# One-hot columns of 128 built as products of a column of 8 and a column of 16

## The chip, the cores and the metric

The kernel runs on one core of one Trainium2 chip. A core has five engines with a queue of instructions each: TensorE (PE, matmuls), VectorE (DVE), ScalarE (ACT), GpSimd (POOL) and SyncE (SP, which issues DMAs). Within one queue instructions run in order; between engines they wait on semaphores. The metric is the time of one execution on the device in microseconds; less is better. The size of an effect is read against the spread of repeated runs of the same kernel.

## The reference, cut to what matters

The program is one layer of a streaming encoder for 1152 tokens (1024 of a prompt, 128 of samples), 9 blocks of 128 tokens. A mixer (projections, band attention, a recurrent branch) is followed by a feed-forward part that retrieves experts: each token chooses 128 of 16384 single-neuron experts (8 heads of 16), and expert number e is a pair (i1, i2) of 128 by 128.

```
def peer_tokens(xt, wq, keys1, keys2, expert_u, expert_v):
    t = xt.shape[0]
    q = (xt @ wq).reshape(t, PEER_HEADS, 2, HALF_KEY)
    s1 = jnp.einsum('thd,hnd->thn', q[:, :, 0], keys1).astype(jnp.float32)
    s2 = jnp.einsum('thd,hnd->thn', q[:, :, 1], keys2).astype(jnp.float32)
    v1, i1 = lax.top_k(s1, TOPK_HALF)
    v2, i2 = lax.top_k(s2, TOPK_HALF)
    cand_s = (v1[..., :, None] + v2[..., None, :]).reshape(t, PEER_HEADS, TOPK_HALF * TOPK_HALF)
    cand_i = (i1[..., :, None] * N_KEYS + i2[..., None, :]).reshape(t, PEER_HEADS, TOPK_HALF * TOPK_HALF)
    top_s, pos = lax.top_k(cand_s, TOPK)
    e_idx = jnp.take_along_axis(cand_i, pos, axis=-1)
    g = jax.nn.softmax(top_s, axis=-1)
    u_sel = expert_u[e_idx]
    act = jax.nn.gelu(jnp.einsum('thkd,td->thk', u_sel, xt).astype(jnp.float32))
    return jnp.einsum('thk,thkd->td', (g * act).astype(xt.dtype), expert_v[e_idx])
```

## The kernel before

The token blocks go through the mixer in three groups, `GROUPS = ((0, 1, SB), (2, 3, 4), (5, 6, 7))`, each with five stages: the recurrent branch, its gates, the attention, the output projections, the retrieval scores. Projections take 24 matmuls each with weights split in a high and a low part; from the second group on the low part comes back from DRAM (lines 163 and 164), so DVE no longer makes it there.

The experts are then applied in two ways. Blocks 0, 5, 6, 7 (`GATHER`) fetch rows of the experts by indirect DMA, one per token and choice (line 910), and DVE takes a dot product (line 937) or adds a scaled row (line 958). Blocks 1, SB, 2, 3, 4 (`DENSE`) run all 16384 experts as matmuls at the end (`dense`), masked by a matrix `G_d` in DRAM that holds each token's weight for each expert. `build_g` makes this matrix; the change is in it.

For one token the matrix of 128 by 128 weights is a product of two sets of one-hot columns: choice k gives a column with a one at i1 and a column with its weight at i2. The table of a block (`tab`: i1, i2 and the weight in three factors `pw`, `hi`, `lo`, with choices on the partitions and tokens along the row) is made by `tables`, stored to DRAM and read back into one buffer. `build_g` handles a block in 4 chunks `c` of 32 tokens, and a chunk in 4 parts `tb` of `OH_T = 8` tokens. A part makes three tiles of 128x1024 (8 tokens of 128 columns), `ow`, `oh` and `ol`, with five DVE instructions, lines 993 to 997:

```
V.tensor_tensor(ow, gp["iota"], row(i2), op=ALU.is_equal)
V.tensor_tensor(ow, ow, row(pw), op=ALU.mult)
V.tensor_tensor(oh, gp["iota"], row(i1), op=ALU.is_equal)
V.tensor_tensor(ol, oh, row(lo), op=ALU.mult)
V.tensor_tensor(oh, oh, row(hi), op=ALU.mult)
```

A 128x1024 tile is laid out as groups of two tokens, 128 columns each, with the two tokens of a group side by side in memory; `row` reads a pair of tokens from the table again for every column. PE multiplies the tiles token by token into PSUM (lines 1008 and 1009), ACT copies the product to a staging tile `st` (line 1011), and after four parts SP stores `st` (2 MB) to `G_d` (line 1013). The three tiles have two buffers each, `st` has one. There are 5 blocks of 4 chunks of 4 parts, 80 parts in all.

Where the parts run is set by a queue `fill` of small steps: in the second and third group `beat` takes steps from it after each projection or attention unit, and likewise steps of the gather of block 0 (`FLOW`). The selection steps of the next blocks (lines 766 to 863, all on DVE) go through the same queue. The order of each engine's instructions is fixed at build time by a list scheduler that goes by a modelled time line. In the attention, one unit on DVE is the bias added to the scores (line 432), their maximum `mx` (line 434) and the reciprocal of the sum (line 439); ACT makes `p` from the maximum (line 437) and scales it by the reciprocal (line 443), and PE's next score matmul (line 524) needs the buffer that line 437 has read.

Of the kernel before, what the change touches and what calls it, by code (L numbers as in the profile page):

```python
# [53 lines left out]
OH_T = 8  # L54
# [15 lines left out]
def kernel(ctx, tc, a):  # L70
# [43 lines left out]
    s_d = [dr_p.tile([8, 128, len(g), 2, 128], F32, name=f"s_d{n}") for n, g in enumerate(GROUPS)]  # L114
    e_d = {b: dr_p.tile([128, 128], I32, name=f"e_d{b}") for b in GATHER}
    g_d = {b: dr_p.tile([128, 128], F32, name=f"g_d{b}") for b in GATHER}
    tab_d = {b: dr_p.tile([128, 320], F32, name=f"tab_d{b}") for b in DENSE}
    x2_d = {b: dr_p.tile([128, D], F32, name=f"x2_d{b}") for b in range(NB)}

    def rstd_of(ss, q_="", r=None):  # L120
        m = sm_p.tile([128, 1], F32, name="rs_m" + q_)
        V.tensor_scalar(m, ss, 1.0 / D, EPS, op0=ALU.mult, op1=ALU.add)
        if r is None:
            r = sm_p.tile([128, 1], F32, name="rs_r" + q_)
        S.activation(r, m, ACTF.Sqrt)
        V.reciprocal(r, r)
        q = sm_p.tile([128, 1], F32, name="rs_q" + q_)
        V.tensor_tensor(q, r, r, op=ALU.mult)
        V.tensor_tensor(q, q, m, op=ALU.mult)
        V.tensor_scalar(q, q, -0.5, 1.5, op0=ALU.mult, op1=ALU.add)  # L130
        V.tensor_tensor(r, r, q, op=ALU.mult)
        return r

    def ssq(x, junk, q_=""):
        ss = sm_p.tile([128, 1], F32, name="ss" + q_)
        S.activation(junk, x, ACTF.Square, accum_out=ss)  # L136
        return ss

# [611 lines left out]

    def table_parts(tab):
        h = tab.bitcast(F16)
        return h[:, 0:128], h[:, 128:256], tab[:, 128:192].bitcast(BF16), h[:, 384:512], h[:, 512:640]

    def select(b, q_=""):

# [119 lines left out]
        def tables(ii, gf):  # L876


            pt = ps_p.tile([128, 4, 128], F32, name="tr", tag="pp")
            for n, src in enumerate((ii[0], ii[1], gf)):  # L880
                T.transpose(pt[:, n, :], src, ident)
            tab = tk.tile([128, 320], F32, name="tab", tag="cand")
            i1, i2, pw, hi, lo = table_parts(tab)
            S.copy(i1, pt[:, 0, :])
            S.copy(i2, pt[:, 1, :])
            wt = tk.tile([128, 128], F32, name="wt", tag="sh")
            S.copy(wt, pt[:, 2, :])
            ma = tk.tile([128, 128], F32, name="ma", tag="m1")
            bits = wt.bitcast(U32)
            V.tensor_scalar(ma.bitcast(U32), bits, 0x007fffff, 0x46000000, op0=ALU.bitwise_and, op1=ALU.bitwise_or)  # L890
            V.tensor_scalar(bits, bits, 0x7f800000, None, op0=ALU.bitwise_and)
            V.tensor_copy(pw, wt)
            S.copy(hi, ma)
            V.tensor_tensor(lo, ma, hi, op=ALU.subtract)
            nc.sync.dma_start(tab_d[b], tab)
# [73 lines left out]
    def build_g(gp, b):  # L969
# [4 lines left out]
        def part(c, tb):  # L974
            def go():
                if c == 0 and tb == 0:
                    make_tables(b)
                    st["t"] = gp["st"].tile([128, 320], F32, name="tab")
                    nc.sync.dma_start(st["t"], tab_d[b])
                if tb == 0:  # L980
                    st["s"] = gp["st"].tile([128, 128, 32], F32, name="st")
                i1, i2, pw, hi, lo = table_parts(st["t"])
                sg = st["s"]
                t = c * 32 + tb * OH_T

                def row(x):
                    return x[:, t:t + OH_T].rearrange("p (g t) -> p g t", t=2).unsqueeze(2).to_broadcast(
                        [128, OH_T // 2, 128, 2])

                ow = gp["oh"].tile([128, OH_T // 2, 128, 2], BF16, name="ow")  # L990
                oh = gp["oh"].tile([128, OH_T // 2, 128, 2], F16, name="oh1")
                ol = gp["oh"].tile([128, OH_T // 2, 128, 2], F16, name="oh2")
                V.tensor_tensor(ow, gp["iota"], row(i2), op=ALU.is_equal)
                V.tensor_tensor(ow, ow, row(pw), op=ALU.mult)
                V.tensor_tensor(oh, gp["iota"], row(i1), op=ALU.is_equal)
                V.tensor_tensor(ol, oh, row(lo), op=ALU.mult)
                V.tensor_tensor(oh, oh, row(hi), op=ALU.mult)
                later.append(lambda: products(c, tb, ow, oh, ol, sg))
                if len(later) > 1:
                    later.popleft()()  # L1000
# [144 lines left out]
    for n, blocks in enumerate(GROUPS):  # L1145
        phase[0] = n
        if n:
            if not gp:
                gp["iota"] = iota = g_p.tile([128, OH_T // 2, 128, 2], F16, name="iota", tag="g5")
                P.iota(iota, pattern=[[0, OH_T // 2], [1, 128], [0, 2]], base=0, channel_multiplier=0,  # L1150
                       allow_small_or_imprecise_dtypes=True)
                gp["st"] = es_g.enter_context(tc.tile_pool(name="st", bufs=1, side="right", reuse_waits="tile"))
                gp["oh"] = es_g.enter_context(tc.tile_pool(name="oh", bufs=2, side="right", reuse_waits="tile"))
            for b in GROUPS[n - 1]:
                if b in DENSE:
# [144 lines left out]
```

## Time and profile before

| what | value |
|---|---|
| median of 3 runs | 3978.68 us (3971.28 to 3997.58) |
| the profiled execution, its own time | 3979.21 us |
| its span, first to last instruction | 3977.3 us |
| busy: PE, PEld (weight loads), DVE, ACT, POOL | 92%, 82%, 77%, 41%, 35% |
| mean granted clock of PE, as a share of 2.4 GHz | 0.967 |
| parts of `build_g` | 80, from 926 to 1994 us |

The span falls into the first group (to about 900 us), the second and third group (to about 2000 us, with all of `build_g` in them) and the dense part with the remaining gathers (to the end). "Busy" is the time in which an engine has an instruction running; waits are listed by the engine that waits and by what it waited for. The granted clock is one of two levels, 1.2 and 2.4 GHz, so a mean of 0.94 says that 12% of the stretch ran at the lower one.

### The profile page before, as it was taken

To read this page: it belongs to the slowest core of one execution; us is meant where nothing else is said; L and a number is where in the kernel's file an instruction comes from. 1 tells how busy PE (TensorE), PEld (TensorE's weight loads), DVE (VectorE), ACT (ScalarE), POOL (GpSimd) and SP (SyncE) were. 2 spreads that over 40 slices of the span, in tenths; PEclk is the share of its full clock that TensorE was granted. 3 is DMA by queue.
4 is the path that set the end of the run, shared out by engine and by line. 5 is a ranking of instruction groups with operands and counts; after the bars stand their busy time and mean duration, and the time that the engine had idled before them with its cause. 6 is when DMAs were issued, how large, how long until landed. Compare 5 with 4: busy or idle time off the path is not lost. (4 is left out here: it accounts for less than half of the span.)

```text
span 3977.3 us, 59539 instructions
## 1 busy us (share of the span) xinstructions
PE 3647.0 (92%) x21775; PEld 3264.7 (82%) x21775; DVE 3042.7 (77%) x6332; ACT 1618.2 (41%) x2699; POOL 1405.4 (35%) x1094
## 2 busy tenths in 40 slices
PE   8998899898998999888888889999999899999998
PEld 7877799876887987778888778888888888888887
DVE  8433357868675879987778888888877887877887
ACT  7554346556644845665532122222222222222222
POOL 0000000122221023222106555655664655655653
PEclk9999999999998999999999999999999999999999
DMA  7778887888899898879968888989888889888986
GB/s 260 253 243 317 296 283 271 327 308 269 316 385 331 294 346 292 292 281 360 379 203 308 306 287 296 320 314 343 311 305 293 322 313 332 311 304 305 331 311 233
DMA packets 470358, 1208.05 MB, mean 304 GB/s; under 512 B 41008, under 2 KB 199088, under 8 KB 467504
## 3 DMA queue, kind: packets, MB, share of 16 engines
q1 hardware_dynamic: 292496, 638.23, 45.2%
q0 software_dynamic: 147456, 536.94, 37.8%
q10 hardware_dynamic: 30112, 29.09, 2.1%
q8 instruction: 170, 2.79, 0.3%
q14 instruction: 124, 1.02, 0.1%
HBM read 1066.15 MB, written 137.94 MB: 303 GB/s over the span
## 5 line engine op out<-in xcount | busy, mean ns | idle before, releaser
L910 POOL DMA_INDIRECT row<-peer_u,ei x512 | 698.0, 1363 | 1260.5 <-DVE row L937 631.3
L910 POOL DMA_INDIRECT row<-peer_v,ei x512 | 683.3, 1334 | 828.7 <-DVE x L958 525.4
L958 DVE SCALAR_TENSOR_TENSOR x<-row,q,x 128x1024 f32<-128x1024 f32 x512 | 655.3, 1280 | 27.2 <-DMA row<-peer_v,ei 20.8
L175 PE MATMUL pp<-xd,hi 128*128 128x320 f32 x2048 | 639.8, 312 | 31.9 <-ACT wf L1043 26.9
L937 DVE SCALAR_TENSOR_TENSOR row<-row,xt 128x1024 f32<-128x1024 f32 x512 | 613.6, 1217 | 66.1 <-DMA row<-peer_u,ei 64.4
L176 PE MATMUL pp<-xd,hi 128*128 128x320 f32 x2048 | 637.5, 311 | 0.3 <-DVE xd L142 0.3
L177 PE MATMUL pp<-xd,lo 128*128 128x320 f32 x2048 | 636.8, 311 | 0.0
L175 PE MATMUL pp<-xn,hi 128*128 128x384 f32 x1344 | 477.4, 356 | 19.1 <-ACT st L1011 7.8
L1069 PE MATMUL S<-vh,wh 128*128 128x512 f32 x1280 | 410.0, 402 | 62.2 <-DVE acc L1077 54.0
L177 PE MATMUL pp<-xn,lo 128*128 128x384 f32 x1344 | 459.4, 343 | 2.1 <-DMA lo<-lo_w_in 2.1
L176 PE MATMUL pp<-xn,hi 128*128 128x384 f32 x1344 | 460.6, 343 | 0.1
L1069 PE MATMUL S<-vh,wl 128*128 128x512 f32 x1280 | 401.1, 402 | 27.6 <-DVE wl L142 27.6
L175 PEld LDWEIGHTS pp<-xd,hi 128*128 128x128 f32 x2048 | 389.9, 190 | 42.6 <-ACT wf L1043 30.7
L141 ACT CAST hi<-raw 128x1024 fp32r<-128x1024 f32 x223 | 233.8, 1049 | 429.0 <-PE pp L176 307.2
L1069 PE MATMUL S<-vl,wh 128*128 128x512 f32 x1280 | 404.0, 397 | 0.0
L176 PEld LDWEIGHTS pp<-xd,hi 128*128 128x128 f32 x2048 | 389.8, 190 | 7.2 <-DVE xd L142 0.6
L177 PEld LDWEIGHTS pp<-xd,lo 128*128 128x128 f32 x2048 | 389.2, 190 | 1.6
L142 DVE TENSOR_TENSOR lo<-raw,hi 128x1024 fp32r<-128x1024 f32 x223 | 271.9, 1220 | 150.1 <-ACT hi L141 134.8
L141 ACT CAST wh<-wf 128x640 fp32r<-128x640 f32 x128 | 93.3, 729 | 616.8 <-DVE wf L1045 583.6
L1069 PEld LDWEIGHTS S<-vh,wh 128*128 128x128 f32 x1280 | 239.3, 193 | 112.3 <-DVE acc L1077 60.9
L163 ACT CAST hi<-raw 128x1024 fp32r<-128x1024 f32 x192 | 200.4, 1047 | 296.5 <-PE pp L176 204.3
L1069 PEld LDWEIGHTS S<-vh,wl 128*128 128x128 f32 x1280 | 246.7, 194 | 84.6 <-DVE wl L142 32.7
(296 smaller groups left out, 6821.7 us busy)
## 6 DMA issues: line engine op xcount, KB each, us to landing
raw<-w_in SPq DMA_DIRECT2D x168, 512.0 KB
raw<-peer_v SPq DMA_DIRECT2D x128, 512.0 KB
raw<-peer_ut SPq DMA_DIRECT2D x127, 512.0 KB
lo<-lo_w_in SPq DMA_DIRECT2D x112, 512.0 KB
G_d<-st SPq DMA_DIRECT2D x20, 2048.0 KB
gt<-G_d SPq DMA_DIRECT2D x32, 1280.0 KB
lo_w_in<-lo SPq DMA_DIRECT2D x56, 512.0 KB
raw<-wq SPq DMA_DIRECT2D x48, 512.0 KB
```

The source lines that it names most:

```text
L141: S.copy(r32(hi), src)
L142: ins = V.tensor_tensor(r32(lo), src, hi, op=ALU.subtract)
L163: S.copy(r32(hi), raw)
L175: T.matmul(out, r32(lh), r32(rh), start=first, stop=False)
L176: T.matmul(out, r32(lh), r32(rl), start=False, stop=False)
L177: T.matmul(out, r32(ll), r32(rh), start=False, stop=last)
L910: P.indirect_dma_start(out=t, out_offset=None, in_=table, in_offset=bass.IndirectOffsetOnAxis(ap=ei[:, j:j + 1], axis=0))
L937: V.scalar_tensor_tensor(u, u, 1.0, xt, op0=ALU.mult, op1=ALU.mult, accum_out=hh[:, j:j + 1])
L958: V.scalar_tensor_tensor(x2, v, q[:, j:j + 1], x2, op0=ALU.mult, op1=ALU.add)
L1069: T.matmul(po[:, m, :], r32(l[:, c1]), r32(r[:, m * 512:m * 512 + 512]), start=(n == 0 and q == 0 and (c == 0 or not held)), stop=(n == EC ...
```

## The change

A number i1 of 0 to 127 is written as 16 times a (0 to 7) plus b (0 to 15). The one-hot column of 128 is the product of a column of 8 at a and a column of 16 at b. `tables` now stores 16 a and b instead of i1 and i2, so `tab` grows from 320 to 448 words a row; the split is integer work on DVE in place of two ACT copies. Once per chunk `build_g` makes the small columns for its 32 tokens in a tile `fac`: four compares and three multiplications by the weight factors, which now go on the columns of 8. Each part makes `ow`, `oh` and `ol` with one product of 128x1024 each. The large counting tile `iota` is replaced by two small ones, and four small statistics tiles get two buffers instead of four.

```
-    tab_d = {b: dr_p.tile([128, 320], F32, name=f"tab_d{b}") for b in DENSE}
+    tab_d = {b: dr_p.tile([128, 448], F32, name=f"tab_d{b}") for b in DENSE}
...
-        m = sm_p.tile([128, 1], F32, name="rs_m" + q_)
+        m = sm_p.tile([128, 1], F32, name="rs_m" + q_, bufs=2)
...
-            tab = tk.tile([128, 320], F32, name="tab", tag="cand")
-            i1, i2, pw, hi, lo = table_parts(tab)
-            S.copy(i1, pt[:, 0, :])
-            S.copy(i2, pt[:, 1, :])
+            tab = tk.tile([128, 448], F32, name="tab", tag="cand")
+            a1, a2, b1, b2, pw, hi, lo = table_parts(tab)
+            for n, (xa, xb) in enumerate(((a1, b1), (a2, b2))):
+                u = tk.tile([128, 128], U32, name="u", tag=("ra", "m3")[n])
+                v = tk.tile([128, 128], U32, name="v", tag="pf")
+                V.tensor_copy(u, pt[:, n, :])
+                V.tensor_scalar(v, u, 15, None, op0=ALU.bitwise_and)
+                V.tensor_copy(xb, v)
+                V.tensor_scalar(u, u, 0x70, None, op0=ALU.bitwise_and)
+                V.tensor_copy(xa, u)
...
                 if tb == 0:
                     st["s"] = gp["st"].tile([128, 128, 32], F32, name="st")
-                i1, i2, pw, hi, lo = table_parts(st["t"])
+
+                    a1, a2, b1, b2, pw, hi, lo = table_parts(st["t"])
+                    st["f"] = fac = g_p.tile([128, 896], F32, name="fac", tag="g5")
+                    h, w = fac.bitcast(F16), fac.bitcast(BF16)
+
+                    def small(x, n):
+                        return x.rearrange("p (g i t) -> p g i t", i=n, t=2)
+
+                    def row(x, n):
+                        return x[:, c * 32:c * 32 + 32].rearrange("p (g t) -> p g t", t=2).unsqueeze(2).to_broadcast(
+                            [128, 16, n, 2])
+
+                    fh, fl, fw = small(h[:, 0:256], 8), small(h[:, 256:512], 8), small(w[:, 512:768], 8)
+                    g1, g2 = small(h[:, 768:1280], 16), small(w[:, 1280:1792], 16)
+                    st["f"] = fh, fl, fw, g1, g2
+                    for n, pairs in ((8, ((fl, a1), (fw, a2))), (16, ((g1, b1), (g2, b2)))):
+                        for o, x in pairs:
+                            V.tensor_tensor(o, gp["iota", n].unsqueeze(1).to_broadcast([128, 16, n, 2]), row(x, n),
+                                            op=ALU.is_equal)
+                    V.tensor_tensor(fw, fw, row(pw, 8), op=ALU.mult)
+                    V.tensor_tensor(fh, fl, row(hi, 8), op=ALU.mult)
+                    V.tensor_tensor(fl, fl, row(lo, 8), op=ALU.mult)
+                fh, fl, fw, g1, g2 = st["f"]
                 sg = st["s"]
-                t = c * 32 + tb * OH_T
-
-                def row(x):
-                    return x[:, t:t + OH_T].rearrange("p (g t) -> p g t", t=2).unsqueeze(2).to_broadcast(
-                        [128, OH_T // 2, 128, 2])
+
+                def product(o, f, g):
+                    gs, full = slice(tb * OH_T // 2, (tb + 1) * OH_T // 2), [128, OH_T // 2, 8, 16, 2]
+                    V.tensor_tensor(o.rearrange("p g (a b) t -> p g a b t", b=16),
+                                    f[:, gs].unsqueeze(3).to_broadcast(full), g[:, gs].unsqueeze(2).to_broadcast(full),
+                                    op=ALU.mult)
...
-                V.tensor_tensor(ow, gp["iota"], row(i2), op=ALU.is_equal)
-                V.tensor_tensor(ow, ow, row(pw), op=ALU.mult)
-                V.tensor_tensor(oh, gp["iota"], row(i1), op=ALU.is_equal)
-                V.tensor_tensor(ol, oh, row(lo), op=ALU.mult)
-                V.tensor_tensor(oh, oh, row(hi), op=ALU.mult)
+                product(ow, fw, g2)
+                product(oh, fh, g1)
+                product(ol, fl, g1)
```

Two places show what becomes of the order. The first is DVE's queue in the attention of the third group, where a chunk's first parts begin. In the names, `x` is the sum of the gather of block 0, `S` the scores, `tab` the table and `fac` the small columns; a number tells one `oh` tile from another. Before:

```order
L434 TENSOR_REDUCE mx<-S 128x1
L993 TENSOR_TENSOR ow<-iota,tab 128x1024
L995 TENSOR_TENSOR oh_18235<-iota,tab 128x1024
L958 SCALAR_TENSOR_TENSOR x_14646<-row,q,x_14646 128x1024
L995 TENSOR_TENSOR oh_18265<-iota,tab 128x1024
L993 TENSOR_TENSOR ow<-iota,tab 128x1024
L994 TENSOR_TENSOR ow<-ow,tab 128x1024
L996 TENSOR_TENSOR oh_18236<-oh_18235,tab 128x1024
L527 MEMSET S 64x64
L958 SCALAR_TENSOR_TENSOR x_14646<-row,q,x_14646 128x1024
L996 TENSOR_TENSOR oh_18266<-oh_18265,tab 128x1024
```

and with the change, where the chunk begins with the set-up (lines 1006 to 1010; line 965 is the gather's add that was line 958):

```order
L142 TENSOR_TENSOR oa<-pp,oa 128x128
L1006 TENSOR_TENSOR fac<-iota_6457,tab 128x256 x2
L1006 TENSOR_TENSOR fac<-iota_6459,tab 128x512 x2
L1009 TENSOR_TENSOR fac<-fac,tab 128x256
L965 SCALAR_TENSOR_TENSOR x_14672<-row,q,x_14672 128x1024
L1008 TENSOR_TENSOR fac<-fac,tab 128x256
L527 MEMSET S 64x64
L1010 TENSOR_TENSOR fac<-fac,tab 128x256
L1016 TENSOR_TENSOR oh_18589<-fac 128x1024
L965 SCALAR_TENSOR_TENSOR x_14672<-row,q,x_14672 128x1024
L1016 TENSOR_TENSOR ow<-fac 128x1024
L432 TENSOR_TENSOR S<-S,bias 128x256
```

The compares of 128x1024 have gone, seven small instructions stand ahead of the chunk's first products, and the gather's adds and the softmax unit's instructions (`S`, `mx`) stand between the pieces as before.

The second place is SP's queue in the output projections of the second group, where the table of the next block is read into its one buffer. `raw` and `lo` are the high and low weights, `G_d<-st` is the store of a finished chunk. Before:

```order
L1013 DMA G_d<-st 128x4096
L164 DMA lo<-lo_w_ba_4883 128x1024
L154 DMA raw<-w_ba 128x1024
L631 DMA tg_d_8098<-tg 128x384
L164 DMA lo<-lo_w_ba_4924 128x1024
L154 DMA raw<-w_ba 128x1024
L631 DMA tg_d_8098<-tg 128x384
L979 DMA tab<-tab_d_128 128x320
```

and with the change:

```order
L986 DMA tab<-tab_d_128 128x448
L154 DMA raw<-w_ba 128x1024
L631 DMA tg_d_8100<-tg 128x384
L164 DMA lo<-lo_w_in_4723 128x1024
L154 DMA raw<-w_ba 128x1024
L631 DMA tg_d_8100<-tg 128x384
L1041 DMA G_d<-st 128x4096
```

The read of the table has moved ahead of the store of the chunk; the last reader of the old table is now the set-up of a block's fourth chunk, where before it was its last part.

On PE nothing is added or removed, and the groups of 16 one-hot matmuls stand at the same projections as before, to within one.

## Rows read from the trace of the kernel before

**Rows 1.** Busy time of each engine in five stretches, their sum; clock, DMA share, GB/s.
```profile
core 0: us, PE busy (x) PEld busy (x) DVE busy (x) ACT busy (x) POOL busy (x), PEclk, DMA share, GB/s
926.00:1060.00 134.00, 120.51 (x818) 98.06 (x817) 109.59 (x241) 85.06 (x162) 30.90 (x29) 0.94 0.80 277
1060.00:1230.00 170.00, 152.56 (x1024) 142.58 (x1021) 117.23 (x235) 85.42 (x126) 34.59 (x33) 0.96 0.98 375
1230.00:1494.00 264.00, 241.79 (x1344) 223.49 (x1344) 194.90 (x726) 154.24 (x239) 36.32 (x33) 0.95 0.89 318
1494.00:1800.00 306.00, 269.76 (x1848) 218.26 (x1847) 272.69 (x643) 191.13 (x366) 83.32 (x75) 0.94 0.83 290
1800.00:1994.00 194.00, 171.81 (x1210) 162.68 (x1211) 144.63 (x302) 100.13 (x135) 41.92 (x33) 0.96 0.97 371
sum 1068.00, PE 956.42 PEld 845.08 DVE 839.04 ACT 615.99 POOL 227.05; mean PE 191.28 PEld 169.01 DVE 167.81 ACT 123.20 POOL 45.41
```

**Rows 2.** Groups on DVE, 926 to 1994 us: count, busy us, mean ns, idle before.
```profile
L995 DVE TENSOR_TENSOR oh<-iota,tab 128x1024 f16<-128x1024 f16 x80 | 54.8, 685 | 52.3 <-PE pg L1008 52.1
...
L997 DVE TENSOR_TENSOR oh<-oh,tab 128x1024 f16<-128x1024 f16 x80 | 54.4, 681 | 0.0
...
L142 DVE TENSOR_TENSOR oa<-pp,oa 128x128 fp32r<-128x128 f32 x37 | 10.5, 284 | 23.1 <-ACT oa L141 23.1
...
L848 DVE TENSOR_TENSOR oh<-oh 128x512 bf16<-128x512 bf16 x16 | 6.6, 415 | 0.0
...
L844 DVE TENSOR_TENSOR oh<-ra,rank 128x1024 bf16<-128x1024 bf16 x8 | 5.4, 678 | 0.0
...
L848 DVE TENSOR_TENSOR oh<-oh 128x256 bf16<-128x256 bf16 x16 | 4.5, 280 | 0.0
...
L142 DVE TENSOR_TENSOR xn<-tr,xn 128x1024 fp32r<-128x1024 f32 x3 | 3.7, 1225 | 15.3 <-ACT xn L141 15.3
...
L890 DVE TENSOR_SCALAR ma<-wt 128x128 uint32<-128x128 uint32 x4 | 0.9, 228 | 2.8 <-ACT wt L887 2.8
...
L829 DVE CAST rb<-sh 128x128 bf16<-128x128 uint32 x3 | 0.7, 219 | 0.0
```

**Rows 3.** The same stretches, line 994 alone: busy us and count.
```profile
926.00:1060.00 134.00, 9.50 (x14) 0.94 0.80 277
...
1494.00:1800.00 306.00, 18.28 (x27) 0.94 0.83 290
```

**Rows 4.** One group on ACT, 926 to 1994 us.
```profile
L884 ACT CAST tab<-tr 128x128 f16<-128x128 f32 x4 | 1.0, 258 | 3.0 <-DVE tp L801 3.0
```

**Rows 5.** What PE waited for, 926 to 1060 us: total, times, longest.
```profile
PE S L524 <- ACT p L437: 4.7, 4, 1.9
...
PE pp L175 <- DVE oa L142: 1.9, 1, 1.9
...
PE pt L453 <- DVE oa L142: 1.2, 1, 1.2
```

**Rows 6.** What PE waited for, 1494 to 1800 us.
```profile
PE S L524 <- ACT p L437: 11.8, 10, 3.2
PE pt L453 <- ACT st L1011: 8.0, 8, 3.3
PE pp L175 <- ACT st L1011: 6.3, 5, 4.1
```

**Rows 7.** What ACT waited for, 926 to 1994 us.
```profile
ACT p L437 <- DVE mx L434: 31.8, 23, 5.8
ACT p L443 <- DVE sum L439: 27.6, 19, 6.5
...
ACT st L1011 <- DMA G_d<-st: 22.1, 7, 5.8
```

**Rows 8.** What SP's queue waited for, 926 to 1994 us.
```profile
SPq L979 <- DVE oh L997: 8.1, 2, 4.8
...
SPq L895 <- DVE tab L894: 7.3, 1, 7.3
```

More of the change, by code (lines that the diff above doesn't have):

```diff
@@ L116 @@
     g_d = {b: dr_p.tile([128, 128], F32, name=f"g_d{b}") for b in GATHER}
-    tab_d = {b: dr_p.tile([128, 320], F32, name=f"tab_d{b}") for b in DENSE}
+    tab_d = {b: dr_p.tile([128, 448], F32, name=f"tab_d{b}") for b in DENSE}
     x2_d = {b: dr_p.tile([128, D], F32, name=f"x2_d{b}") for b in range(NB)}
     def rstd_of(ss, q_="", r=None):
-        m = sm_p.tile([128, 1], F32, name="rs_m" + q_)
+        m = sm_p.tile([128, 1], F32, name="rs_m" + q_, bufs=2)
         V.tensor_scalar(m, ss, 1.0 / D, EPS, op0=ALU.mult, op1=ALU.add)
         if r is None:
-            r = sm_p.tile([128, 1], F32, name="rs_r" + q_)
+            r = sm_p.tile([128, 1], F32, name="rs_r" + q_, bufs=2)
         S.activation(r, m, ACTF.Sqrt)
         V.reciprocal(r, r)
-        q = sm_p.tile([128, 1], F32, name="rs_q" + q_)
+        q = sm_p.tile([128, 1], F32, name="rs_q" + q_, bufs=2)
         V.tensor_tensor(q, r, r, op=ALU.mult)
@@ L134, in ssq @@
     def ssq(x, junk, q_=""):
-        ss = sm_p.tile([128, 1], F32, name="ss" + q_)
+        ss = sm_p.tile([128, 1], F32, name="ss" + q_, bufs=2)
         S.activation(junk, x, ACTF.Square, accum_out=ss)
@@ L752, in table_parts @@
         h = tab.bitcast(F16)
-        return h[:, 0:128], h[:, 128:256], tab[:, 128:192].bitcast(BF16), h[:, 384:512], h[:, 512:640]
+        return (h[:, 0:128], h[:, 128:256], h[:, 640:768], h[:, 768:896], tab[:, 128:192].bitcast(BF16), h[:, 384:512],
+                h[:, 512:640])
     def select(b, q_=""):
@@ L977, in go @@
                     make_tables(b)
-                    st["t"] = gp["st"].tile([128, 320], F32, name="tab")
+                    st["t"] = gp["st"].tile([128, 448], F32, name="tab")
                     nc.sync.dma_start(st["t"], tab_d[b])
@@ L1148 @@
             if not gp:
-                gp["iota"] = iota = g_p.tile([128, OH_T // 2, 128, 2], F16, name="iota", tag="g5")
-                P.iota(iota, pattern=[[0, OH_T // 2], [1, 128], [0, 2]], base=0, channel_multiplier=0,
-                       allow_small_or_imprecise_dtypes=True)
                 gp["st"] = es_g.enter_context(tc.tile_pool(name="st", bufs=1, side="right", reuse_waits="tile"))
+                for k, m in ((8, 16), (16, 1)):
+                    gp["iota", k] = gp["st"].tile([128, k, 2], F16, name=f"iota{k}")
+                    P.iota(gp["iota", k], pattern=[[m, k], [0, 2]], base=0, channel_multiplier=0,
+                           allow_small_or_imprecise_dtypes=True)
                 gp["oh"] = es_g.enter_context(tc.tile_pool(name="oh", bufs=2, side="right", reuse_waits="tile"))
```

## The prediction

> **What bounds the kernel now.** The one-hot parts run from 926 to 1994 us, so I read that stretch first, cut where the kinds of work change: attention of the second group (926 to 1060), its output projections and scores (1060 to 1230), the recurrent branch and gates of the third group (1230 to 1494), its attention (1494 to 1800) and its output (1800 to 1994) [rows 1]. PE is busy for 956 of 1068 us, DVE for 839. In the two attention stretches together, 440 us, DVE is busy for 109.6 + 272.7 = 382.3 us, 87%, and PE for 390.3, so PE stands idle for 49.7 us. In the two output stretches DVE is at 69% and 75%, while the DMA engines are at 0.98 and 0.97 [rows 1]: there is little for a faster DVE to give there. So the question is how much of PE's idle time in the attention DVE causes.
>
> The second view is what PE waited for. In the attention the waits that lead back to DVE are those for `p` (line 437, which needs DVE's maximum) and for `oa`: 4.7 + 1.9 + 1.2 us in the first stretch and 11.8 in the second, 19.6 us in all [rows 5, 6]. The other large ones there, 8.0 and 6.3 us, are for the copy of the product to `st` [rows 6], and `st` itself waits for its store to DRAM, 22.1 us over the whole stretch [rows 7], which the change doesn't touch. ACT's own waits for the maximum and the reciprocal are larger, 31.8 and 27.6 us [rows 7], but most of that never reaches PE. In the other direction, DVE is idle for 52.1 us before line 995 because PE hasn't yet released the one-hot buffers [rows 2].
>
> **The change, part by part.** Durations are those of the profiled execution (3979.2 us, half a microsecond from the median of 3978.7).
>
> Removed from DVE: five groups of 80 instructions of 128x1024, of which the first and last by cost take 54.8 and 54.4 us [rows 2]; the five sum to 272.8 us, 0.682 each.
>
> Added, products: 240 instructions of 128x1024. Both inputs of a product are read repeatedly (the column of 8 sixteen times over, the column of 16 eight times), with the two tokens of a pair side by side. The nearest row is the compare of line 844, whose two inputs are both re-read, 0.678 us; the removed ones, with one re-read input whose run is a pair, take the same, so 0.682 is taken: 163.7 us. The far end is an instruction of the same size that doesn't go at this pace, 1.225 us [rows 2]; it belongs to the third rival.
>
> Added, set-up: per chunk five instructions of 256 and two of 512 elements. The rows of those sizes take 0.280 and 0.415 us [rows 2], so 2.23 us a chunk and 44.6 us for 20.
>
> Added, tables: ten instructions of 128x128 per block. Two read PSUM (0.284 as the row that subtracts from PSUM), four are integer logic (0.228), four convert from integers (0.219) [rows 2]: 2.36 us a block, 11.8 us for five. ACT loses two copies a block, 0.26 us each [rows 4], 2.6 us in all, hidden under PE's work.
>
> Net on DVE: 272.8 - 163.7 - 44.6 - 11.8 = 52.7 us less. PE's instructions, ACT's copies and the stores to `G_d` are as before.
>
> Where it falls: 14 + 27 = 41 of the 80 parts run in the attention stretches [rows 3], so 52.7 x 41/80 = 27 us less DVE work there. DVE's idle time in those 440 us goes from 57.7 to about 85 us.
>
> What PE gets from it is the uncertain step. Its bounds are 0 (every microsecond freed is spent waiting for PE's buffers) and 27 (DVE sets the pace all through). I choose by the waits: the 19.6 us that lead back to DVE should shrink roughly as DVE's idle time grows, to 57.7/85 = 0.68 of it, so by 6.3 us. PE's clock adds to this. Its granted mean is 0.94 in both attention stretches [rows 1], so 12% of 440 us, 53 us, ran at 1.2 GHz, and work that PE does there takes twice as long: about 26 us are lost. If that shrinks as PE's idle time does, by 6.3/49.7, it gives 3.3 us. For the remaining 628 us, with 26 us less DVE work but PE and DMA in front, I take 2 us between 0 and 5. Sum: 6.3 + 3.3 + 2 = 12 us.
>
> Costs to set against it. The table's store waits in SP's queue for the last of the ten instructions; it comes 2.36 - 0.52 = 1.8 us later, five times 9 us at most. Weight loads stand behind it in that queue, where one such store has already waited 7.3 us for DVE [rows 8]. Cover: four buffers of raw weights, so that a load which is issued 2 us later still lands in time; without the cover the end is 9 us later. Against this, the read of the next table no longer waits for a block's last part (8.1 us in SP's queue [rows 8]), since the set-up of its fourth chunk is the last reader. The set-up puts up to 2.23 us ahead of a softmax maximum once per chunk, but the part behind it is 1.36 us shorter (two instructions less), so the first unit is delayed by at most 0.9 us and the following ones are earlier. The new waits inside a chunk (product for set-up, set-up for table) are on DVE itself, where order alone keeps them, or for a table that is read earlier. The statistics tiles with two buffers instead of four serve chains of which hardly two are under way at once; zero, and under 2 us if not.
>
> The dense part is the same in work, and the order of the gathers within it is nearly the same; it begins earlier by what the stretch gains. Forecast: 3979.2 - 12 = 3967 us; for this case alone 3953 to 3976.
>
> **The rivals.** *It was hidden.* PE is the bound nearly everywhere (956 of 1068 us), and DVE gives the freed time back in the wait for the one-hot buffers, 52.1 us before, 100 after. For it: this wait is already DVE's longest there, and in the output stretches it is PE's and the DMA engines' pace that counts. Against: PE does wait 16.5 us for `p` in the attention. Time: 3979, with the tables' 9 us 3976 to 3988. The Trainium skill (Perfetto Trace Analysis, section Identifying the Most-Contended Engine) says that a kernel gets faster by work on its most contended engine; that is PE here, so by that rule nothing is gained. The trace agrees for the output stretches and not quite for the attention, where DVE's 382 us of 440 stand beside PE's 390.
>
> *DVE set the pace.* If DVE's queue is what holds the attention units, all 52.7 us come off: 3926 us, and 3926 to 3945 with a part of it hidden. For it: 89% busy from 1494 to 1800, and the 59 us that ACT waits for DVE's softmax results [rows 7]. Against: PE's idle time in attention is only 49.7 us, and 14.3 of the 26 us listed for the second stretch are for `st` [rows 6]; half of the removed work lies outside the attention.
>
> *The products are slow.* The gain needs a product at the removed instructions' pace. If reading both columns repeatedly costs the fast pace, a product takes 1.225 us [rows 2], 0.543 more; 240 of them add 130 us, and DVE has 78 us more to do than before. 40 of those 78 us fall in the attention, where DVE would then be busy for 96%: 4019 us if these count alone, 4057 if all of it does. The point that decides is a product of (272.8 - 44.6 - 11.8)/240 = 0.90 us: above it DVE has more work than before. Against it stand line 844 with two re-read inputs, and the removed lines with pairs, all at 0.68 [rows 2]. The Trainium skill (Vector Engine (DVE) Microarchitecture Reference, section 5.1) has the rule behind this rival: two-source instructions on 16-bit data go two elements a cycle where every innermost step is 1, and one element read 16 times in succession was seen to run at one a cycle. By that rule the pair of tokens decides: the innermost run is two neighbours, so the products should be fast. The rows agree: lines 995 and 997 re-read a pair 128 times at 0.68 us.
>
> **How the numbers follow.** Chances: forecast 0.59, hidden 0.22, DVE set the pace 0.13, slow products 0.06. The range leaves out the slow products and about half of the third case, and holds the tables' 9 us above: 3935 to 3988. One per cent, 40 us, is about what a measurement of this kernel can tell from no change (three runs lie within 26 us). Faster by more than that needs nearly all of the DVE work to come off the path: 0.10. Slower by more: the slow products, 0.06. Within: 0.84.
>
> **What would show it.** Products at 0.68 us, x240, and the set-up at 0.28 and 0.42, x100 and x40; DVE's busy time from 926 us to the end of the parts down by about 50 us; in the attention the waits of PE for `p` down from 16.5 to about 11 us; DVE's wait for the one-hot buffers up from 52 us; the granted clock in the attention slightly above 0.94; the dense part as long as before. The forecast is wrong if the attention stretches shorten by more than 20 us, if the wait for `p` stays while DVE's wait for PE takes up the rest, if products stand near 1.2 us, or if the dense part changes its length by more than 10 us, which nothing in this argument provides for.

## The result and the profile after

The changed kernel took 4003.6 us (median of 8 runs, 3993.9 to 4012.2), the kernel before 3979.7 beside it (8 runs, 3964.6 to 3997.6): a ratio of 1.0056, interval 1.0039 to 1.0072. It is 24 us slower, and above the range of the prediction. The profiled run of the changed kernel is its slowest, 4012.2 us; its span is 4010.5, that of before 3977.3.

First the head of the page, busy time by engine, of the kernel before and of the changed one.

```profile
PE 3647.0 (92%) x21775; PEld 3264.7 (82%) x21775; DVE 3042.7 (77%) x6332; ACT 1618.2 (41%) x2699; POOL 1405.4 (35%) x1094
```

```profile
PE 3680.7 (92%) x21775; PEld 3298.4 (82%) x21775; DVE 2996.8 (75%) x6362; ACT 1620.9 (40%) x2689; POOL 1393.2 (35%) x1095
```

DVE has 45.9 us less, as intended. PE has the same 21775 matmuls and is busy for 33.7 us longer. Span less busy time, PE's idle time, is 330.3 us before and 329.8 after. So in these two traces the whole difference, 33 us between the spans, is matmuls that take longer; no wait has grown in sum.

The new instructions, as groups on DVE (parts and set-up, 926 to 2030 us of the changed kernel), answer to [rows 2]:

```profile
L1016 DVE TENSOR_TENSOR oh<-fac 128x1024 f16<-128x1024 f16 x160 | 109.0, 686 | 66.6 <-PE pg L1036 60.8 <-PE pg L1037 4.7 <-PE pt L453 0.9
L1016 DVE TENSOR_TENSOR ow<-fac 128x1024 bf16<-128x1024 bf16 x80 | 54.5, 684 | 0.0
L1006 DVE TENSOR_TENSOR fac<-iota,tab 128x512 bf16<-128x512 f16 x20 | 8.4, 422 | 0.0
...
L1006 DVE TENSOR_TENSOR fac<-iota,tab 128x256 f16<-128x256 f16 x20 | 5.7, 285 | 4.9 <-DMA tab<-tab_d 4.6
...
L892 DVE CAST tab<-u 128x128 f16<-128x128 uint32 x8 | 2.2, 277 | 0.0
```

Products, set-up and tables cost what was forecast. DVE now waits 60.8 + 4.7 us for PE to release the one-hot buffers, before 52.1 [rows 2].

What PE waited for, in the kernel before (926 to 1994 us) and in the changed one (926 to 2030 us): total, times, longest.

```profile
PE pp L175 <- ACT hi L163: 23.4, 15, 4.8
PE S L524 <- ACT p L437: 17.1, 15, 3.2
PE pp L175 <- ACT st L1011: 13.8, 12, 5.1
PE pg L1008 <- ACT st L1011: 13.2, 18, 2.3
PE pt L453 <- ACT st L1011: 8.2, 9, 3.3
```

```profile
PE pp L175 <- ACT hi L163: 20.4, 12, 5.2
PE pg L1036 <- ACT st L1039: 16.6, 19, 5.4
PE pp L175 <- ACT st L1039: 13.0, 11, 4.9
PE S L524 <- ACT p L437: 10.7, 11, 3.6
PE pt L453 <- ACT st L1039: 10.0, 8, 4.9
```

The wait for `p` has shrunk by 6.4 us, that for the cast of the weights (line 163) by 3.0. Part of that comes back in the waits for ACT's copies to `st`, 4.4 us more.

Where the time went is read from windows that end at the same point of the work in both (at the first, 49th, 85th, 121st, 145th, 166th and 185th cast of line 163, and at the seventh step of the dense part). Columns as in [rows 1]. The kernel before:

```profile
0.00:618.00 618.00, 551.75 (x3822) 498.27 (x3823) 303.39 (x758) 318.70 (x649) 24.15 (x70) 0.97 0.79 274
...
896.00:1176.00 280.00, 256.08 (x1729) 220.02 (x1727) 218.53 (x477) 160.51 (x277) 63.27 (x60) 0.96 0.89 320
...
1401.00:1571.00 170.00, 158.20 (x883) 135.66 (x884) 143.19 (x521) 76.01 (x145) 44.57 (x44) 0.94 0.92 326
1571.00:1816.00 245.00, 216.72 (x1577) 177.55 (x1576) 208.13 (x401) 158.84 (x294) 63.41 (x54) 0.96 0.83 291
1816.00:1927.00 111.00, 100.37 (x707) 95.56 (x707) 87.64 (x145) 57.54 (x73) 28.55 (x20) 0.97 0.98 378
...
2122.00:3977.00 1855.00, 1739.68 (x9479) 1568.21 (x9477) 1541.02 (x2063) 453.88 (x643) 1076.29 (x752) 0.97 0.87 307
```

The changed kernel:

```profile
0.00:627.00 627.00, 563.51 (x3826) 509.11 (x3827) 303.91 (x762) 319.48 (x649) 18.61 (x71) 0.96 0.78 271
...
906.00:1194.00 288.00, 260.79 (x1724) 223.86 (x1725) 203.81 (x495) 160.89 (x272) 61.53 (x59) 0.95 0.87 312
...
1421.00:1599.00 178.00, 162.33 (x881) 138.53 (x882) 145.84 (x531) 75.65 (x145) 46.08 (x44) 0.92 0.89 313
1599.00:1840.00 241.00, 221.49 (x1578) 182.06 (x1577) 191.32 (x414) 160.08 (x288) 59.74 (x54) 0.93 0.84 297
1840.00:1957.00 117.00, 105.90 (x725) 100.42 (x724) 78.50 (x141) 58.69 (x74) 27.59 (x22) 0.96 0.95 358
...
2152.00:4010.00 1858.00, 1738.10 (x9484) 1569.14 (x9482) 1542.09 (x2060) 453.88 (x643) 1077.28 (x755) 0.97 0.86 308
```

Two things stand out. In the first 620 us none of the changed arithmetic runs, and yet PE is busy 11.8 us longer there for the same matmuls, to within four. In most of the third group's attention (1571 to 1816 us before) the stretch is 4 us shorter and PE's idle time falls from 28 to 20 us, which is a gain of the predicted kind; but the granted clock falls from 0.96 to 0.93, and PE is busy for 5 us more. Most of the rest is lost around the second group's attention (896 to 1176 us before, 8 us longer), in the stretch from 1401 us (8 us longer) and in that from 1816 us (6 us longer). The dense part is as long as before, within 3 us.

### The profile page after: what moved, and what is told of

It reads as the page before. It is cut to its first block, busy times and chain, and to the rows that moved or that the text cites. A ratio compares the mean times of both kernels' runs of the same rounds, so it can differ in the third digit from the quotient of the medians.

```text
span 4010.5 us, 59580 instructions
## 1 busy us (share of the span) xinstructions
PE 3680.7 (92%) x21775; PEld 3298.4 (82%) x21775; DVE 2996.8 (75%) x6362; ACT 1620.9 (40%) x2689; POOL 1393.2 (35%) x1095
## 5 line engine op out<-in xcount | busy, mean ns | idle before, releaser
L175 PE MATMUL pp<-xn,hi 128*128 128x384 f32 x1344 | 482.7, 360 | 17.7 <-ACT st L1039 5.4
L176 PE MATMUL pp<-xn,hi 128*128 128x384 f32 x1344 | 465.7, 346 | 0.6 <-DVE xn L142 0.5
```

Of the source, the lines that this page charges most:

```text
L175: T.matmul(out, r32(lh), r32(rh), start=first, stop=False)
L176: T.matmul(out, r32(lh), r32(rl), start=False, stop=False)
```

## Experiments

Three theories stood at the start. **Order:** the list scheduler lays out all engines anew for any edit, and the 24 us are what this one layout happens to cost; other layouts of the same change cost other amounts. **Tables and set-up:** the additions cost more than their sum. **Load:** less work on DVE itself slows PE. They were to be told apart by other orders of both kernels, by taking parts of the change away, and by changing DVE's work alone. In the texts on record below they are theory O or 1 (order), T or 3 (tables and set-up) and W or 2 (load); in those on `PROJ_US` 4.0 and `TAB_LATE` 8, W stands for any cost of the change's own work.

**Sixteen orders of the two kernels.** Two constants shift where steps are put without changing any work: `TAB_LATE` (9: the place in `fill` at which a block's tables are put) and `PROJ_US` (3.9: the length of a projection unit that `beat` reckons with). Both kernels were run with each value.

```
-PROJ_US = 3.9
+PROJ_US = 4.0
...
-TAB_LATE = 9
+TAB_LATE = 10
```

Expected of `TAB_LATE` 10, before and after:

> The kernel before with one number changed that moves no work in or out: a block's table is queued ten steps of fill later instead of nine, so the order of PE, DVE and SP is made anew from there. Theory O (the loss of 24 us comes from the re-made order: PE's pauses fall elsewhere, the sum of its idle time is unchanged, and it spends some 45 us more at 1.2 GHz): any re-made order scatters by about as much as the change itself, so 3965 to 4005 us, not 3980 again, and the mean clock moves with the time. Theory T (tables and set-up cost the time) and theory W (less DVE work itself is what slows PE): this kernel stays within 8 us of 3980.

> The changed kernel with the same number changed (table ten steps later instead of nine). Theory O: the order is new once more, so the time is free to land anywhere from 3960 to 4010 us and is as likely to lie below 3995 as above. Theories T and W: the same work is still there, so within 8 us of 4003.

Of `PROJ_US` 4.0:

> The kernel before with the planning time of a projection set to 4.0 us instead of 3.9; it only shifts the points at which steps of fill are taken, so the work is the same and the order is made anew. Theory O (the order sets the difference, the work hardly any): 3965 to 4005 us; together with the other orders of the same work it gives a scatter of some 10 us around a mean near 3985. Theory W (the change's work costs 24 us): within 8 us of 3980.

> The changed kernel with the same planning time of 4.0 us. Theory O: 3965 to 4005 us, as the kernel before with the same number within 20 us either way. Theory W: within 8 us of 4003, 24 above the kernel before with this number. Prediction on record: 12 us below the kernel before with this number.

Of `TAB_LATE` 8:

> The kernel before with a block's table queued after eight steps instead of nine; the same work in another order. Theory O: 3965 to 4005 us. Theory W: within 8 us of 3980.

> The changed kernel with a block's table queued after eight steps. Theory O: 3965 to 4010 us, and the mean of the changed kernel over its orders (nine, ten, eight steps, other pace) within 10 us of the mean of the kernel before over the same four. Theory W: within 8 us of 4003. If the DVE work saved is worth the 12 us of the prediction, the mean over the four orders lies 12 us below.

Of `PROJ_US` 4.1:

> The kernel before with PROJ_US at 4.1 instead of 3.9: the work is the same, the scheduler's plan and so the order are another. Theory 1 (order): within 3965 to 3995, as its other orders. Theories 2 and 3 say nothing of it beyond no change, 3980.

> The changed kernel with PROJ_US at 4.1 instead of 3.9, another order of the same work. Theory 1 (order): within 3970 to 4005, and the mean of the five orders of the changed kernel within 0.3% of that of the five orders of the kernel before. Theories 2 and 3: the change's cost of 24 us stands in this order too, 4004.

Of `PROJ_US` 3.8:

> The kernel before with PROJ_US at 3.8, a further order of the same work. Theory 1 (order): 3970 to 3995, as the five orders so far (3975 to 3991).

> The changed kernel with PROJ_US at 3.8, the partner of the kernel before it. Theory 1 (order): 3970 to 4005. If the freed 52.7 us of VectorE are worth what the forecast gave them, the mean over all pairs of orders must come out 12 us below that of the kernel before; if they are worth nothing, within 5 us of it; if the change costs time in itself, above.

Of `PROJ_US` 3.7 and 4.2:

> The kernel before with PROJ_US at 3.7. Theory 1 (order): 3970 to 3995.

> The changed kernel with PROJ_US at 3.7. Theory 1 (order): 3970 to 4005; over all pairs, 12 us below the kernel before if the forecast's gain is there, within 5 us of it if the freed time is worth nothing, above if the change costs time in itself.

> The kernel before with PROJ_US at 4.2. Theory 1 (order): 3970 to 3995.

> The changed kernel with PROJ_US at 4.2. Theory 1 (order): 3970 to 4005; over all pairs as said of the pair at 3.7.

Measured: the median, the ratio to the kernel before on the same chip with its interval, and from each profile the busy time of PE, its idle time (span less busy), the granted clock and the start of the first cast of line 163 (us). The median is over 8 to 12 runs; the last four columns are of one run each, which lies up to 16 us from its median.

| order | kernel | median | ratio | PE busy | idle | clock | first cast |
|---|---|---|---|---|---|---|---|
| as given | before | 3979.7 | 1 | 3647.0 | 330.3 | .967 | 617.8 |
| | after | 4003.6 | 1.0056 [1.0039, 1.0072] | 3680.7 | 329.8 | .960 | 626.5 |
| TAB_LATE 10 | before | 3990.8 | 1.0021 [1.0007, 1.0035] | 3646.7 | 334.8 | .965 | 622.6 |
| | after | 3985.0 | 1.0005 [.9990, 1.0020] | 3669.8 | 313.4 | .961 | 624.6 |
| PROJ_US 4.0 | before | 3983.6 | .9997 [.9980, 1.0014] | 3652.7 | 312.5 | .962 | 620.4 |
| | after | 3973.0 | .9969 [.9956, .9982] | 3673.8 | 301.7 | .961 | 626.2 |
| TAB_LATE 8 | before | 3975.0 | .9983 [.9967, .9999] | 3641.4 | 323.6 | .967 | 620.7 |
| | after | 4000.9 | 1.0043 [1.0029, 1.0057] | 3677.4 | 329.2 | .959 | 626.6 |
| PROJ_US 4.1 | before | 3990.7 | 1.0016 [.9997, 1.0035] | 3657.8 | 328.1 | .959 | 625.0 |
| | after | 3975.3 | .9982 [.9966, .9999] | 3662.2 | 308.6 | .965 | 626.0 |
| PROJ_US 3.8 | before | 3975.7 | .9979 [.9961, .9997] | 3634.3 | 332.8 | .965 | 620.6 |
| | after | 3981.4 | .9992 [.9979, 1.0004] | 3658.2 | 317.5 | .966 | 623.0 |
| PROJ_US 3.7 | before | 3976.6 | .9992 [.9980, 1.0004] | 3651.2 | 319.4 | .964 | 615.8 |
| | after | 3981.6 | 1.0004 [.9983, 1.0025] | 3653.3 | 331.3 | .966 | 626.8 |
| PROJ_US 4.2 | before | 3981.7 | .9995 [.9974, 1.0015] | 3663.4 | 322.3 | .957 | 617.8 |
| | after | 3988.4 | 1.0005 [.9989, 1.0020] | 3667.9 | 325.9 | .960 | 625.8 |

The order theory holds for most of the 24 us. The same change spans 3973 to 4004 us over eight orders, the same unchanged work 3975 to 3991. The mean ratio is 0.9998 before and 1.0007 after; from the scatter between orders (0.0015 and 0.0029) the difference of 0.0009 is uncertain by 0.0012, so the change as such costs 4 us, give or take 5. The forecast gain of 12 us (0.0030) isn't there, and neither is a loss of 24. The other two theories asked for about 4003 us of the changed kernel in every order, give or take 8; six of the eight lie below 3990.

The clock goes with the order. Averaged over all of its runs, the granted clock of the changed kernel is 0.9605 and 0.9606 in its two slow orders (`TAB_LATE` 8 and as given) and 0.962 to 0.964 in the six faster ones; the kernel before lies between 0.9577 (`PROJ_US` 4.1) and 0.9642 (`TAB_LATE` 8). Whether the lower clock costs the time, or the same pauses cost both, these runs don't tell apart.

Where an order loses is read from two of the changed kernel that lie far apart. With `TAB_LATE` 8 (4000.9 us), windows of the same kind, from the 49th to the 85th cast of line 163, from the 121st by way of the 145th to the 166th, and from the 185th to the dense part's seventh step:

```profile
906.00:1199.00 293.00, 263.34 (x1729) 225.25 (x1730) 206.57 (x517) 159.96 (x271) 65.42 (x59) 0.95 0.84 306
...
1422.00:1600.00 178.00, 165.44 (x879) 141.69 (x880) 141.83 (x488) 76.90 (x149) 45.56 (x44) 0.89 0.87 311
1600.00:1843.00 243.00, 223.08 (x1582) 182.20 (x1580) 194.24 (x455) 160.29 (x286) 58.82 (x54) 0.92 0.83 298
...
1957.00:2149.00 192.00, 163.39 (x991) 149.69 (x990) 146.42 (x539) 74.79 (x104) 29.25 (x24) 0.94 0.74 271
```

and with `PROJ_US` 4.0 (3973.0 us):

```profile
908.00:1187.00 279.00, 260.12 (x1726) 222.41 (x1726) 207.31 (x500) 160.47 (x273) 66.25 (x62) 0.96 0.89 326
...
1408.00:1583.00 175.00, 161.58 (x879) 139.04 (x880) 139.88 (x485) 75.24 (x144) 44.69 (x44) 0.93 0.89 315
1583.00:1823.00 240.00, 219.52 (x1563) 177.52 (x1562) 193.80 (x438) 157.19 (x286) 60.85 (x55) 0.94 0.84 302
...
1941.00:2126.00 185.00, 160.30 (x956) 148.39 (x957) 139.65 (x533) 74.18 (x104) 21.69 (x19) 0.92 0.72 261
```

The work and DVE's share of it are the same. Of the 31 us between the spans 14 arise around the second group's attention, where PE is idle for 30 us against 19; 6 in the third group's, where the clock is 0.89 and 0.92 against 0.93 and 0.94 and PE is busy for 7.4 us more (388.5 against 381.1); 7 in the last window and 8 in the dense part (1857 against 1849); the windows not shown take 4 back. There is no one place; pauses and the clock share it.

**The tables as before.** The changed kernel with tables that hold i1 and i2 again, copied by ACT in rows of 320 words; the numbers aren't split, so both small columns are compared with the whole i1 and i2, and the weights come out wrong.

```
-                V.tensor_copy(u, pt[:, n, :])
-                V.tensor_scalar(v, u, 15, None, op0=ALU.bitwise_and)
...
+            S.copy(a1, pt[:, 0, :])
+            S.copy(a2, pt[:, 1, :])
```

> The changed kernel with the tables as they were before the change: two copies on ACT instead of ten DVE instructions per block, and rows of 320 words. The numbers are not split, so the small columns compare whole expert numbers and the weights matrix is not the reference's; instructions and sizes of the rest are those of the change. Theory T: the ten instructions and the later store of the table are the cost, so 10 us or more come back: 3993 us or less. Theory W: no difference but the 12 us of DVE work, 3998 to 4010. Theory O: a new order, 3965 to 4010 without a rule.

It took 3984.3 us, ratio 1.0012, interval 1.0000 to 1.0024. By itself that would speak for the tables. But the changed kernel with the new tables takes 3985.0 with `TAB_LATE` 10, and less in four other orders: taking the tables away does no more than another order.

**The set-up once per block.** The later three chunks of a block use the first one's columns, so their weights are wrong; `fac` is taken once per block too.

```
+                    if c == 0:
+                        st["fac"] = g_p.tile([128, 896], F32, name="fac", tag="g5")
...
+                    if c == 0:
+                        for n, pairs in ((8, ((fl, a1), (fw, a2))), (16, ((g1, b1), (g2, b2)))):
```

> The changed kernel, with the seven set-up instructions of a chunk issued only for the first chunk of a block (5 times instead of 20, 33 us less on VectorE); the later chunks use the first one's columns, so that they multiply with the wrong weights. Theory 1 (order): anywhere between 3970 and 4004, no closer to 3980 than other orders came. Theory 2 (a freed VectorE slows TensorE): above 4004. Theory 3 (the set-up costs it): 24 us times three quarters less, about 3986 or below.

It took 3988.0 us, ratio 1.0015, interval 0.9999 to 1.0032, within the spread of the orders. It is near what the set-up theory asked for (3986 or below), but that theory can't explain 3973 with the whole set-up.

**Less work on DVE, without the change.** Three of the five instructions of a part are kept; the multiplications by `pw` and `hi` are left out.

```
-                V.tensor_tensor(ow, ow, row(pw), op=ALU.mult)
...
-                V.tensor_tensor(oh, oh, row(hi), op=ALU.mult)
```

> The kernel before with three of the five instructions of each part: the multiplications of one column set by the weight pw and of one by hi are left out, so the weights matrix is not the reference's. DVE has 160 x 0.682 = 109 us less to do, twice the net saving of the change, without set-up and without new tables. Prediction on record: about twice its gain, 3979 - 24 = 3955 us. Theory W (less DVE work slows PE): slower than 3990. Theory T: faster than 3965, since nothing is added. Theory O: anywhere from 3950 to 4000, with DVE's saving visible only in its own idle time.

It took 3966.2 us, ratio 0.9960, interval 0.9945 to 0.9974: with 109 us fewer of instructions on DVE (its busy time falls by 90.9 us, to 2951.8), 14 us less, 0.13 us for each. The theories asked for more than 3990 (load), less than 3965 (tables and set-up) and 3950 to 4000 (order); the prediction's own rate asked for 3955. A freed DVE doesn't slow PE, and it gives little. It is one order, though, and by the scatter of the orders of before (0.0015, 6 us) the 14 us are uncertain by at least that.

**More work on DVE, with the change.** Two of the three products of a part are issued twice.

```
                 product(ow, fw, g2)
                 product(oh, fh, g1)
+                product(ow, fw, g2)
+                product(oh, fh, g1)
```

> The changed kernel, with the products into ow and oh1 issued a second time in each part (same values, same tiles), so that a part has five instructions of 128x1024 as before the change: 160 more of 0.684 us, 109 us more on VectorE, 57 us more than the kernel before has. Theory 1 (the order that the scheduler lays out decides, VectorE's load matters little): between 3973 and 4020, since leaving out 109 us of VectorE work gained 14 us earlier, so that adding as much costs about that on top of what the new order happens to give. Theory 2 (a freed VectorE slows TensorE): at or below 3980, at least 20 us below the changed kernel's 4004. Theory 3 (the set-up and the tables cost it): about 4004 to 4020, never below 3995, since both are still there.

It took 4007.4 us, ratio 1.0063, interval 1.0040 to 1.0087: 4 us above the changed kernel in its given order, and 21 above the mean of its eight orders, for 109 us of instructions on DVE (its busy time rises by 88.3 us). One order can't say which of the two is the cost. The load theory, which asked for 3980 or less, falls. That it lies in the range of the set-up theory, 4004 to 4020, is no support for that one, for the reason given above.

**What the traces of all these runs show together: a slower matmul.** The column of first casts is the surprise. Before this cast none of the changed arithmetic runs, though the statistics tiles with two buffers are in use, and the order is nearly the same; still it comes at 615.8 to 625.0 us in the kernels of before (mean 620.1) and at 623.0 to 626.8 in the eight orders after (mean 625.7). The three kernels of the changed form that aren't in the table come at 619.7 (old tables), 621.8 (set-up once) and 620.4 (five products), so this cast alone doesn't separate the forms. What does is the pace of single matmuls, in a stretch in which PE is never idle and the clock is 1.0. One 64 us window each: the kernel before, and before with `PROJ_US` 4.0,

```profile
473.00:537.00 64.00, 64.00 (x371) 64.00 (x371) 36.29 (x50) 24.98 (x32) 0.00 (x0) 1.00 0.81 291
```

```profile
476.00:540.00 64.00, 64.00 (x365) 64.00 (x363) 35.59 (x49) 23.86 (x31) 0.00 (x0) 1.00 0.82 293
```

and the changed kernel:

```profile
477.00:541.00 64.00, 64.00 (x364) 64.00 (x363) 38.95 (x54) 24.17 (x31) 0.00 (x0) 1.00 0.84 295
```

There are two paces. Between the 69th and the 85th cast of `raw` on line 141, 384 matmuls of lines 175 to 177 take 66.60 us or 67.88 us in all twenty traces, 173.4 or 176.8 ns each, and nothing between. Of the nine kernels of the form before (with the one of three instructions) five show the faster pace in this stretch; of the eleven of the changed form none. It isn't this stretch alone: from start to start of successive matmuls of these lines (those under 230 ns, averaged over each 100 us up to 2000 us) the changed form has 176.5 to 177.1 ns in every trace, the kernel before 173.4 to 175.1, and its form in the other eight traces 173.3 to 176.6. The groups of lines show it too, for the same 64 matmuls of those windows, before and after (count, busy us, mean ns):

```profile
L176 PE MATMUL pp<-mg,hi 128*128 128x384 f32 x64 | 21.5, 336 | 0.0
```

```profile
L176 PE MATMUL pp<-mg,hi 128*128 128x384 f32 x64 | 21.7, 339 | 0.0
```

Before the dense part 6912 of these matmuls run, some 6150 of them back to back like this; at 2.4 ns each (176.7 against 174.3) those are 15 us. Of the 11.8 us up to the first cast they are about 6 (some 2090 of them at 2.7 ns); by the rate found below, 14 us more at 1.2 GHz make another 4. The table gives the same from another side: over its sixteen profiles, a straight line through PE's busy time and the time at 1.2 GHz (span x 2 x (1 - clock)), with an offset for the changed form, puts that offset at 15.8 us, uncertain by 2.5, and a microsecond at the lower clock at 0.29 us (uncertain by 0.05).

These are single runs, and they set the forms further apart than the medians do: their spans differ by 12.8 us in the mean, the medians by 4. The spans of all recorded runs of the sixteen kernels, averaged for each kernel and fitted in the same way, put the changed form 6 us above the kernel before at equal time at 1.2 GHz, uncertain by 3; the traces alone, with 15.8 us of pace and 5.8 less idle time, say 10. So the slower pace is seen in every trace of the changed form, but what it costs in the median run is less sure than its 16 us.

What of the change does this is argued, not shown. It is there before any of the changed arithmetic has run, in every order, with the old tables as well, with the set-up issued once, and with five products. It isn't the chip: with `PROJ_US` 4.0 and with `TAB_LATE` 8 the kernel before ran on one chip, in the stretch above at the slower pace and at the faster one. One thing that all eleven share and the nine don't have, and that is in force so early, is the size of the statistics tiles of `rstd_of` and `ssq`: two buffers instead of four. The pools of the inputs of these matmuls (`xn`, `oa`, `mg`) are opened behind that of these tiles, so the inputs may lie elsewhere in memory. The kernel before with the two-buffer lines alone, in which no instruction would change its place, would tell; it wasn't run. Nor does the place explain why the kernel before has both paces, in different stretches of one trace and, with another order, in the same stretch.

## Why the prediction was wrong

**DVE's terms: right.** Products 0.684 to 0.686 us against 0.682, set-up 0.28 and 0.42, tables 12.6 us against 11.8, DVE's busy time down by 45.9 us in the whole span against 52.7. The slow products, the last rival, are refuted.

**What PE gets: right in kind, smaller.** The wait for `p` in the attention was to fall from 16.5 to 11 us and fell to 8.8. The two stretches in the changed kernel, 926 to 1060 and 1536 to 1840 us:

```profile
PE S L524 <- ACT p L437: 3.3, 3, 2.0
```

```profile
PE S L524 <- ACT p L437: 5.5, 5, 3.6
```

The waits for `oa`, which the same step counted among those to shrink (3.1 us [rows 5]), have grown to 5.7 in the first of these stretches:

```profile
PE pp L175 <- DVE oa L142: 3.2, 1, 3.2
PE pt L453 <- DVE oa L142: 2.5, 2, 2.3
```

With `oa` the sum forecast to fall by 6.3 us, from 19.6, fell by about 5. Over eight orders PE's mean idle time goes from 325.5 to 319.7 us, 5.8 less (uncertain by 4.7), where 6.3 + 2 were forecast. In the order as given 0.5 us are left of it: PE waits 4.4 us more for `st` (the three rows sum to 39.6 us, those of before to 35.2), and the gain of the third group's attention is lost again elsewhere.

**The step that failed first: "PE's instructions, ACT's copies and the stores to `G_d` are as before".** They are the same in number and not in duration. A term for slower matmuls, 16 us by the traces, is missing from the sum, and it is larger than the whole gain of 12. The statistics tiles were priced by waits alone, at zero; whether they cause the slower matmuls stays open.

**The step that failed second: the clock.** 3.3 us were to come back, with a clock slightly above 0.94 in the attention. In the changed kernel it is 0.94 in that of the second group (936 to 1072 us) and 0.93 in that of the third (1512 to 1820). Over the whole span it is 0.960 against 0.967; in the two traces 65 us more ran at 1.2 GHz, and at 0.29 us for each that is 19 us. With the 15.8 us of the pace this makes about 34, against the 33.7 by which PE is busy longer. The rate that the prediction took was too high as well: half of the time at 1.2 GHz was to be lost. Back-to-back matmuls of 128x384 start every 320 ns there (the median of 236 in the trace of before), against 174 at the full clock, so 0.46 is the most, and 0.29 is what the sixteen profiles show. Idle time as such doesn't set the clock here: in the two traces it fell in the third group's attention while the clock fell too.

**The 24 us of the medians.** Part of the 65 us is which run was profiled: at 0.967 the profile of before has a higher clock than most runs of that kernel, whose mean over the 142 recorded beside the other kernels is 0.9638; the changed kernel's mean over eight is 0.9606. By the means 27 us more ran at 1.2 GHz, which is 8 us. With 16 for the pace and nothing gained in idle time that adds up to the 24 measured. It is an account that fits, not one that an experiment has taken apart.

**The range** allowed for nothing but the change's own costs. That a new layout alone moves a kernel, with no work changed, wasn't in it: from 7 us below its mean to 9 above for the kernel before, and from 13 below to 17 above for the changed one. Five of the eight orders of the changed kernel lie within 3935 to 3988; that the one as given is the slowest of them is bad luck on top of the wrong steps, not part of them. Of the rivals "it was hidden" comes nearest in the mean (1.0007), and by the traces for another reason than it gave: not that nothing was gained, but that the gain was spent on slower matmuls.

**A version that beats both.** The changed kernel with `PROJ_US` 4.0 took 3973.0 us, ratio 0.9969, interval 0.9956 to 0.9982. This is a choice among orders, and is not evidence for the change.

## What to carry to other kernels

Where a scheduler lays out the program, time a few layouts of both versions, by constants that change no work, before an effect of half a per cent is put down to an edit. Compare first the busy time of the bounding engine for the same instructions, also in stretches that the edit doesn't touch; what an edit changes in passing, here a few buffer counts, can't be priced at nothing without that. A small gain on an engine off the path has to be set against both.

## What was unexpected of the hardware

Matmuls of 128x384, back to back at the full clock, ran at one of two paces, 173.4 or 176.8 ns; in the stretch of 384 each trace kept to one of them, and eleven kernels showed the slower one in every 100 us up to 2000 us, one trace each. The cause stays open.

The granted clock varies between runs of one kernel (0.957 to 0.966 in the ten of before with `PROJ_US` 4.2) about as much as between the sixteen profiles (0.957 to 0.967), so a single profile says little of it; the means over all runs still differ between orders of the same work, 0.958 to 0.964. In two traces it fell from 0.96 to 0.93 while PE's idle time fell from 28 to 20 us in the third group's attention. What in an order decides it stays open.
